# A two-layer encoder on one core: the second sequence's attention norm moved beside the first projection, norms issued in portions, and two pools ordered per layer

## The chip, the cores and the metric

The kernel runs on one core of one Trainium2 chip. Its time is the device time of that core in microseconds, and a version is compared with another by the median of its runs. TensorE is PE in the rows (PEld is its weight load), VectorE is DVE, ScalarE is ACT, GpSimd is POOL, SyncE is SP. A letter q behind an engine's name stands for its queue.

## The reference

Two sequences of 512 tokens, each 1024 wide (`x_prompt` and `x_sample`), go through the same two layers with the same weights; each has a condition vector of its own. In short:

```python
for i in range(2):
    sh1, sc1, g1, sh2, sc2, g2 = adaln(c, mod_w[i], mod_b[i])   # silu(c) @ w + b, six rows
    h = rmsnorm(x, norm1_g[i]) * (1 + sc1) + sh1
    m = retention(h, ...) if i == 0 else attention(h, ...)
    x = x + g1 * m
    h = rmsnorm(x, norm2_g[i]) * (1 + sc2) + sh2
    x = x + g2 * (square(relu(h @ mlp_w1[i])) @ mlp_w2[i])
return rmsnorm(x, final_g)
```

Layer 0's mixer is a retention with 4 heads (keys 256 wide, values 512 wide, with a decay in both directions, a group norm and a gate). Layer 1's is attention with 8 query heads and 2 key/value heads of 128, with a norm and a rotation of queries and keys. The hidden width of the feed-forward part is 4096. All of it is float32.

## The kernel before, in words

Activations lie transposed, as eight tiles of 128 x 512 (features on the partitions, tokens along the free axis). Each float32 operand of a matmul is cut in two: `hi`, its copy in the short format, and `lo`, the rest, so that one product is three matmuls (`mm3`, L221 to L223: hi with hi, hi with lo, lo with hi). `split` (L225) and `load_piece` (L203) make the cuts: ACT copies, DVE subtracts. Weights come in pieces of 128 x 1024 from DRAM on SP's queue into a raw tile and are then cut. One projection of the attention (`Att.proj`) is four pieces, each used in 24 matmuls, into four PSUM banks.

The program is written out in one order by hand, and a scheduler places it on the engines; each engine runs its instructions in the order it got. `issue_after` and `high_priority` bend that order. Generators (`run`, `weave`, `zipped`, `part`) put the parts of one job between the parts of another.

The stages, in order of time:

- **Retention, steps 0 to 7** (L1215 on): head n of sequence s in step 4s + n. Step 3 also makes the norm of sequence 1 (`nm`, 8 modulated tiles, each with a fetch of x on POOL's queue through `xfp`, three tiles), and step 7 the second norm of sequence 0. `nm.a` is the sum of squares, the root and a diagonal; `nm.c` spreads the diagonal with ones (a matmul into a bank); `nm.m` makes the eight modulated tiles. In step 7 they are made by `modulate_keep`, which also writes each to DRAM. Beside all steps the rows of `adaln` are made by dots on DVE (L385), whose weights are fetched on POOL's queue into the pools f2p (8 tiles) and xfp; the two halves of each condition row (`cb`) and the rotation tables also live in f2p. What is left of the dots is done by `flush` at the end of step 7.
- **The wide stage of layer 0** (`wide_stage`, L902): it closes the mixer's pools and opens sf, su, wh (eight cut weight tiles of 2 KB a partition) and sq (three raw tiles of 4 KB), one behind the other in the memory that the mixer's pools and f2p had. With `reuse_waits="tile"` a new tile waits for the old tiles at its place, not for the whole old pool. Its matmuls are those of the feed-forward part, combined over pairs of pieces and the two sequences with seven products in place of eight (`seven`).
- **The attention** (L1299 on): `nm` is the norm of sequence 0, made between the last down projections of layer 0; `p2, p0, p1` are its projections (2 is keys and values, 0 and 1 the queries), `q2, q0, q1` those of sequence 1, and `nm1` the norm of sequence 1. `a0.heads()` and `a1.heads()` run the heads, and `fill` gives each of their steps a piece of other work. Before, `nm1` is made by the filler of `a0.heads()` and q2 and q0 follow in it; q1 stands behind the heads.
- **The wide stage of layer 1**, the last down projections and the final norm.

The banks of PSUM: "a" four, and "m" four outside the attention, where "s" and "t" have two each instead. `mbank()` gives an "m" bank, or an "a" bank where there is no "m". The pool rp holds 48 tiles for cut activations, fp 12 for plain ones.

Of the kernel before, what the change touches and what calls it, by code (L numbers as in the profile page):

```python
# [22 lines left out]
SQ_W = 8  # L23
SQ_RAW = 3
# [6 lines left out]
def kernel(  # L31
# [84 lines left out]
    def bank(t):  # L116
        return ps[t].tile([P, T], F32, tag=t, name="p" + t)

    def mbank():
        return bank("m") if "m" in ps else abank()  # L120

    def ptile():
# [5 lines left out]
    def abank():  # L128
        return psa.tile([P, T], F32, tag="a", name="pa")
# [29 lines left out]
    def bg_until(n):  # L159
        while len(bg) + len(loaded) > n:  # L160
            bg_dot()
            bg_load()
# [9 lines left out]
    def flush():  # L172
        bg_until(0)

    sq = {}
# [72 lines left out]
    def fetch(src, alloc=xtile, eng=nc.gpsimd):  # L248
        t = alloc()
        eng.dma_start(t, src)  # L250
        return t

    class Stats:
# [26 lines left out]
        def spread(self, dg, sb=False):  # L280
            bc = mbank()
            mm(bc, ones, dg, start=True, stop=True)
            if not sb:
                return bc
            bs = ftile()
            act(bs, bc, AF.Copy)
            return bs
# [17 lines left out]
    def stats_of(tiles):  # L305
        st = Stats()
        for x in tiles:
            st.add(x)
        return st
# [69 lines left out]
    modc = {}  # L379
# [520 lines left out]
    wide_pools = ExitStack()  # L900

    def wide_stage(m, st1):  # L902
        mixer.close()
        sq["f"] = wide_pools.enter_context(tc.tile_pool(name="sf", bufs=SQ_F, reuse_waits="tile"))
        sq["s"] = wide_pools.enter_context(tc.tile_pool(name="su", bufs=SQ_SUM, reuse_waits="tile"))
        sq["w"] = wide_pools.enter_context(tc.tile_pool(name="wh", bufs=SQ_W, reuse_waits="tile"))
        sq["p"] = wide_pools.enter_context(tc.tile_pool(name="sq", bufs=SQ_RAW, reuse_waits="tile"))
        nm = Norm(st1, lambda k: m.x[1][k], modc[m.L, 4, 1], modc[m.L, 3, 1], True, keep=hparks[m.L][1])
        m.h[1] = nm.h
        wide = Wide(m, hparks[m.L], hhparks[m.L], lambda i, k: sqtile if i == 6 or (i == 5 and k < 3) else rtile)  # L910
        wide.negate()
        steps = ([("d", 0, i) for i in range(4)] + [("u", 1, f) for f in range(4)]
                 + [("d", 1, i) for i in range(4)])
        load = lambda q: m.w1(0, q[2]) if q[0] == "u" else m.w2(0, q[2])
        hand_over = {0: [nm.a], 1: [nm.c, lambda: nm.m(4)], 2: [nm.m], 3: [lambda: wide.h_fetch(0)],
                     4: [lambda: wide.h_fetch(1)], 5: [lambda: wide.h_forms(0)], 6: [lambda: wide.h_fetch(2)],
                     7: [lambda: wide.h_forms(1)], 8: [lambda: wide.h_fetch(3), lambda: wide.h_forms(2)],
                     9: [lambda: wide.h_forms(3)]}
        w = load(steps[0])
        for n, (kind, s, i) in enumerate(steps):  # L920
            nxt = load(steps[n + 1]) if n + 1 < len(steps) else None
            if kind == "u":
                if i == 0:
                    m.hh[s] = []
                m.up(w, s)
            else:
                m.down(w, i, s, lambda o, s=s: nc.gpsimd.dma_start(park[s][o], m.x[s][o]))
            w = nxt
            for f in hand_over.get(n, ()):
                f()  # L930
        wide_mlp(wide, m)
# [165 lines left out]
    def run(g, n=None):  # L1097
        while n is None or n > 0:
            try:
                next(g)  # L1100
            except StopIteration:
                return
            if n is not None:
                n -= 1
# [19 lines left out]
    r = Ret(0, x0, [])  # L1124
# [28 lines left out]
    for i in range(4):  # L1153
        for t in range(2):
            k = 2 * i + t
# [58 lines left out]
    m = mlps[0]  # L1214
    for step in range(8):  # L1215
        s, n = divmod(step, 4)
        nm = None
        r.scores(n, strip)
        if step == 3:
            with tc.issue_after(first_pool.ins):  # L1220
                s1 = stats_of(fetch(xs[1][k]) for k in range(KD))
            nm = Norm(s1, lambda k: fetch(xs[1][k]),
                      modc[0, 1, 1], modc[0, 0, 1], True)
            r1 = Ret(1, None, nm.h)
        if step == 7:
            nm = Norm(stats_of(fetch(park[0][k]) for k in range(KD)), lambda k: fetch(park[0][k]),
                      modc[0, 4, 0], modc[0, 3, 0], True, keep=hparks[0][0])
            m.h[0] = nm.h
        if step > 0:
            r.v(n)  # L1230
        if nm is not None:
            nm.a()
        r.g(n, [0] if step else [3])
        if nm is not None:
            nm.c()
        r.y(n)
        if nm is not None:
            nm.m()
        if step < 7:
            strip = decay_strip((n + 1) % 4)  # L1240
        if step == 7:
            r.g(n, [1, 2, 3])
        if step < 7:
            nxt = r1 if step == 3 else r
            n1 = (n + 1) % 4
            for t in (ORDER if step else ORDER_FIRST).split():
                i = int(t[1])
                if t[0] == "q":
                    nxt.qk(n1, i)
                elif t[0] == "z":  # L1250
                    r.tz([i])
                else:
                    r.g(n, [i])
            if step == 0:
                flush()
                for ch in (1, 0, 2):
                    mod_chunk(cb, 0, ch, (1,), True)
                for ch in (4, 3, 5):
                    mod_chunk(cb, 0, ch, alt=ch == 5)
                for ch in (1, 0, 2, 3, 4, 5):  # L1260
                    mod_chunk(cb, 1, ch, alt=ch < 5)
            if step < 7:
                pace[0] = PACE[step]
            if step == 2:
                bg_until(80)
            if step == 3:
                bg_until(72)
            if step == 6:
                bg_until(48)
            if step == 3:  # L1270
                r.out(n, lambda o: nc.gpsimd.dma_start(park[0][o], x0[o]))
                r1.x = [fetch(xs[1][k], ptile) for k in range(KD)]
                r = r1
            else:
                r.out(n)
        else:
            m.x[1] = r.x
            m.ups(0, 0, [0])
            r.tz([0, 1])
            m.ups(0, 0, [1])  # L1280
            r.tz([2, 3])
            m.ups(0, 0, [2])
            st1 = Stats()
            r.out(n, lambda o: st1.add(r.x[o]))
            with tc.issue_after(r.last.ins):
                m.x[0] = [fetch(park[0][k], ftile, nc.scalar) for k in range(KD)]
            m.ups(0, 0, [3])
            flush()
    f2_ctx.__exit__(None, None, None)
    wide_stage(m, st1)  # L1290
    st = [Stats(), Stats()]

    def parker(s):
        def after(o):
            st[s].add(m.x[s][o])
            nc.gpsimd.dma_start(park[s][o], m.x[s][o])
        return after

    run(m.downs(7, 0, parker(0)))  # L1299
    nm = Norm(st[0], lambda k: m.x[0][k], modc[1, 1, 0], modc[1, 0, 0], True)  # L1300
    d = m.downs(7, 1, parker(1))
    run(d, 1)
    nm.a()
# [15 lines left out]
    nm1 = Norm(st[1], lambda k: fetch(park[1][k]), modc[1, 1, 1], modc[1, 0, 1], True)  # L1319
    a1 = Att(1, nm1.h, tabs)  # L1320
    p2, p0, p1 = a0.proj(2), a0.proj(0), a0.proj(1)
    q2, q0, q1 = a1.proj(2), a1.proj(0), a1.proj(1)

    def part(g, n):
        for _ in range(n):
            run(g, 1)
            yield

    def zipped(g, h):
        for _ in range(3):  # L1330
            run(h, 1)
            yield
            run(g, 1)
            yield
        run(g)
        run(h, 1)
        yield

    run(p2, 4)
    run(zipped(p2, p0))  # L1340
    run(zipped(p0, p1))

    def fill():
        h1 = nm1.steps(4)
        for i in range(4):
            run(p1, 1)
            run(h1, 1)
            yield
        run(p1)
        run(h1)  # L1350
        yield from part(q2, 4)
        yield from zipped(q2, q0)

    f = fill()
    weave(a0.heads(), f)
    run(f)
    m = mlps[1]
    st = [Stats(), Stats()]
    with tc.issue_after(a0.last.ins):
        run(q0)  # L1360
    o0 = a0.out(park[0], park[2], st[0])
    run(q1, 4)
    run(o0, 1)
    run(q1, 1)
    run(o0, 1)
# [1 line left out]
    nm = Norm(st[0], lambda k: fetch(park[2][k]), modc[1, 4, 0], modc[1, 3, 0], True, keep=hparks[1][0])  # L1367
# [17 lines left out]
    psm_ctx = banks_of(m=4)  # L1385
    psm_ctx.__enter__()
    wide_stage(m, st[1])

    def finish(s, st):
# [7 lines left out]
    st = [Stats(), Stats()]  # L1397
# [161 lines left out]
```

## Time and profile before

| | |
|---|---|
| median of 3 runs | 2591.9 us (2591.0 to 2595.68) |
| the profiled execution | 2592.08 us |
| its span, first to last instruction | 2590.3 us |
| mean granted clock of TensorE | 0.988 |
| PE busy with matmuls | 2505.1 us, 97% |
| DVE, ACT, POOL busy | 77%, 43%, 20% |

A stretch in which PE is busy for less than its length is idle time of PE; a granted clock of 0.50 is the lower of TensorE's two levels (1.2 GHz against 2.4 GHz). Times in rows count from the span's start.

### The profile page before, as it was taken

How to read it: one execution, taken by the hardware profiler on the slowest of the kernel's cores; microseconds unless marked ns; L12 is line 12 of the kernel's file. 1: busy time of each engine (PE TensorE's matmuls, PEld its weight loads, DVE VectorE, ACT ScalarE, POOL GpSimd, SP SyncE). 2: the span in 40 equal slices, each digit the busy share in tenths (PEclk: the TensorE clock that was granted, in tenths of full speed). 3: DMA queues.
4: the chain of work that ended last, by engine and by line, in shares of the span. 5: the costliest groups of instructions: out<-in, count | busy, mean ns of one | idle time of the engine just before them, and what ended most of it. 6: DMA issues, size and time to landing. Idle time of an engine off the chain costs nothing.

```text
span 2590.3 us, 32585 instructions
## 1 busy us (share of the span) xinstructions
PE 2505.1 (97%) x11186; PEld 2048.7 (79%) x11186; DVE 1993.7 (77%) x3800; ACT 1119.1 (43%) x1949; POOL 525.2 (20%) x947
## 2 busy tenths in 40 slices
PE   6999999999999989999999999899999999999998
PEld 4878888778888777888888887688787788888887
DVE  6777687789989778666888876877766767688877
ACT  3333234232333445444533344776754444454423
POOL 2212212231231112221421110000114122142100
PEclk9999999999999999999999999999999999999999
DMA  7544544555556456444754343223347544485423
GB/s 251 191 146 153 169 134 157 192 170 179 161 179 187 152 181 199 163 163 150 246 195 139 124 143 107 66 66 102 92 152 263 165 161 157 153 276 171 143 89 106
DMA packets 133994, 414.00 MB, mean 160 GB/s; under 512 B 21250, under 2 KB 24194, under 8 KB 133828
## 3 DMA queue, kind: packets, MB, share of 16 engines
q0 software_dynamic: 68352, 224.58, 25.8%
q1 hardware_dynamic: 59284, 180.32, 22.3%
q10 hardware_dynamic: 6192, 7.02, 0.8%
q8 instruction: 88, 1.44, 0.2%
q14 instruction: 78, 0.64, 0.1%
HBM read 332.15 MB, written 79.69 MB: 159 GB/s over the span
## 4 chain that ended last, share of the span: by engine, by line
PE 67%; issue 12%; DVE 9%; DMA 6%; POOL 4%; ACT 1%; POOLq 0%; SPq 0%; ACTq 0%; DVEq 0%
PE pm L222 6%; PE pm L223 6%; PE pm L221 6%; PE pa L671 6%; PE pa L669 6%; PE pa L670 6%; PE pa L222 5%; PE pa L223 5%; PE pa L221 5%; PE pm L671 4%; PE pm L670 4%; PE pm L669 4%; DVE junk L385 2%; POOL hhpark L761 1%; DMA f<-in_modw_dram 1%
## 5 line engine op out<-in xcount | busy, mean ns | idle before, releaser
L208 ACT ACTIVATE whi<-raw 128x1024 fp32r<-128x1024 f32 x174 | 183.8, 1058 | 337.5 <-PE pm L222 152.8
L221 PE MATMUL pm<-r,whi 128*128 128x512 f32 x768 | 302.8, 397 | 11.7 <-ACT r L1176 5.8
L222 PE MATMUL pm<-r,whi 128*128 128x512 f32 x768 | 301.0, 392 | 3.4 <-DVE r L316 2.8
L223 PE MATMUL pm<-r,wlo 128*128 128x512 f32 x768 | 300.3, 391 | 0.0
L209 DVE TENSOR_TENSOR wlo<-raw,whi 128x1024 fp32r<-128x1024 f32 x174 | 213.4, 1227 | 100.0 <-ACT whi L208 97.5
L228 ACT ACTIVATE wh<-rawq 128x512 fp32r<-128x512 f32 x228 | 141.9, 629 | 286.1 <-PE pm L670 157.3
L228 ACT ACTIVATE wh<-sum 128x512 fp32r<-128x512 f32 x208 | 129.7, 629 | 279.8 <-PE pa L670 170.8
L669 PE MATMUL pa<-r,wh 128*128 128x512 f32 x624 | 243.0, 389 | 2.5 <-ACT wh L228 2.5
L671 PE MATMUL pa<-r,wh 128*128 128x512 f32 x624 | 243.0, 389 | 2.0 <-DVE wh L229 2.0
L670 PE MATMUL pa<-r,wh 128*128 128x512 f32 x624 | 242.7, 389 | 0.0
L671 PE MATMUL pm<-r,wh 128*128 128x512 f32 x468 | 182.1, 389 | 0.0
L670 PE MATMUL pm<-r,wh 128*128 128x512 f32 x468 | 182.1, 389 | 0.0
L669 PE MATMUL pm<-r,wh 128*128 128x512 f32 x468 | 182.1, 389 | 0.0
L221 PEld LDWEIGHTS pm<-r,whi 128*128 128x128 f32 x768 | 145.7, 190 | 44.4 <-ACT r L1176 6.2
L222 PE MATMUL pa<-wlo,r 128*128 128x512 f32 x440 | 174.9, 397 | 4.7 <-DVE wlo L209 4.7
L221 PE MATMUL pa<-whi,r 128*128 128x512 f32 x440 | 173.3, 396 | 2.8 <-ACT whi L208 1.5
L223 PE MATMUL pa<-whi,r 128*128 128x512 f32 x440 | 174.1, 396 | 0.0
L385 DVE SCALAR_TENSOR_TENSOR junk<-f,f 128x512 bf16<-128x512 f32 x224 | 156.4, 698 | 22.3 <-DMA f<-in_modw_dram 19.3
L222 PEld LDWEIGHTS pm<-r,whi 128*128 128x128 f32 x768 | 145.3, 189 | 35.4 <-DVE r L316 3.7
L229 DVE TENSOR_TENSOR wh<-sum,wh 128x512 fp32r<-128x512 f32 x208 | 141.6, 685 | 39.4 <-ACT wh L228 38.0
L229 DVE TENSOR_TENSOR wh<-rawq,wh 128x512 fp32r<-128x512 f32 x228 | 155.2, 683 | 21.8 <-ACT wh L228 21.5
L223 PEld LDWEIGHTS pm<-r,wlo 128*128 128x128 f32 x768 | 145.0, 189 | 30.4
(277 smaller groups left out, 6008.7 us busy)
## 6 DMA issues: line engine op xcount, KB each, us to landing
rawq<-in_w_dram SPq DMA_DIRECT2D x144, 512.0 KB, 3.9
raw<-in_wri_dram SPq DMA_DIRECT2D x92, 512.0 KB, 3.7
r<-hhpark POOLq DMA_DIRECT2D x142, 256.0 KB, 4.4
f<-in_modw_dram POOLq DMA_DIRECT2D x128, 256.0 KB, 3.5
hhpark<-f POOLq DMA_DIRECT2D x96, 256.0 KB, 2.9
hhpark<-p POOLq DMA_DIRECT2D x88, 256.0 KB, 2.3
xf<-in_modw_dram POOLq DMA_DIRECT2D x80, 256.0 KB, 3.5
raw<-in_wro_dram SPq DMA_DIRECT2D x32, 512.0 KB, 4.0
```

Source lines behind the costliest of these rows:

```text
L208: act(hi, raw, AF.Copy)
L209: ins = tt(lo, raw, hi.bitcast(F32), ALU.subtract)
L221: mm(ps, a[0], b[0], start=first, stop=False)
L222: mm(ps, a[0], b[1], start=False, stop=False)
L223: return mm(ps, a[1], b[0], start=False, stop=last)
L228: split.last = act(hi, src_f32, AF.Copy)
L229: split.dve = tt(lo, src_f32, hi.bitcast(F32), ALU.subtract)
L385: stt(junk, w[hf], 0.5, cb[hf], ALU.mult, ALU.mult, accum_out=a[:, 2 * k + hf:2 * k + hf + 1])
L669: mm(ps, a[0], b[0], start=first and k == 0, stop=False, **more)
L670: mm(ps, a[0], b[1], start=False, stop=False, **more)
L671: mm(ps, a[1], b[0], start=False, stop=k == n - 1, **more)
L761: nc.gpsimd.dma_start(out[i - 1], t)
```

## The change

Five edits.

1. **Pools of the wide stage.** In layer 0 the raw tiles' pool is opened before that of the cut weight tiles; in layer 1 the order stays (cut weight tiles first).
2. **Portions.** In steps 3 and 7 `nm.m` makes three tiles at a time: three after `r.y`, and three more after each of the gates `g1` and `g2` (the last two after the second of them); before, all eight follow `r.y`.
3. **The norm of sequence 0 at the attention's start** makes tiles 2, 4 and 6 with `modulate_pool`: POOL multiplies x with the spread root, ACT makes hi and the full value with scale and bias, DVE subtracts.
4. **`nm1` moves** from the filler of the heads to between the four quarters of p2. Its diagonal and its spread use a "t" bank (`home`).
5. **The heads' filler**: each of the first four steps takes a step of p1's tail and a quarter of q2; then p1's rest, q2's tail zipped with q0, and three quarters of q1. Behind the heads one quarter of q1 is left where four were.

```diff
+    home = []
+
     def mbank():
+        if home:
+            return bank(home[0])
         return bank("m") if "m" in ps else abank()
...
-        sq["w"] = wide_pools.enter_context(tc.tile_pool(name="wh", bufs=SQ_W, reuse_waits="tile"))
-        sq["p"] = wide_pools.enter_context(tc.tile_pool(name="sq", bufs=SQ_RAW, reuse_waits="tile"))
+        for q, bufs in (("w", SQ_W), ("p", SQ_RAW))[::1 if m.L else -1]:
+            sq[q] = wide_pools.enter_context(tc.tile_pool(name="sq" + q, bufs=bufs, reuse_waits="tile"))
...
         r.y(n)
         if nm is not None:
-            nm.m()
+            nm.m(3)
         if step < 7:
             strip = decay_strip((n + 1) % 4)
         if step == 7:
-            r.g(n, [1, 2, 3])
+            for i in (1, 2, 3):
+                r.g(n, [i])
+                nm.m(3)
...
                 else:
                     r.g(n, [i])
+                    if nm is not None:
+                        nm.m(3)
...
-    nm = Norm(st[0], lambda k: m.x[0][k], modc[1, 1, 0], modc[1, 0, 0], True)
+    nm = Norm(st[0], lambda k: m.x[0][k], modc[1, 1, 0], modc[1, 0, 0], True, (2, 4, 6))
...
-    run(p2, 4)
+    run(p2, 1)
+    home.append("t")
+    nm1.a()
+    run(p2, 1)
+    nm1.c()
+    home.clear()
+    nm1.m(4)
+    run(p2, 1)
+    nm1.m()
+    run(p2, 1)
     run(zipped(p2, p0))
     run(zipped(p0, p1))
 
     def fill():
-        h1 = nm1.steps(4)
         for i in range(4):
             run(p1, 1)
-            run(h1, 1)
+            run(q2, 1)
             yield
         run(p1)
-        run(h1)
-        yield from part(q2, 4)
         yield from zipped(q2, q0)
+        yield from part(q1, 3)
...
-    run(q1, 4)
+    run(q1, 1)
     run(o0, 1)
```

## Rows read from the trace of the kernel before

**Rows 1.** The page, part 1: busy us (share of the span) xinstructions.

```profile
PE 2505.1 (97%) x11186; PEld 2048.7 (79%) x11186; DVE 1993.7 (77%) x3800; ACT 1119.1 (43%) x1949; POOL 525.2 (20%) x947
```

**Rows 2.** The waits of PE: us in total, times, longest us.

```profile
PE pm L221 <- ACT wh L228: 6.8, 1, 6.8
...
PE pa L222 <- DVE wlo L209: 4.7, 2, 4.2
```

**Rows 3.** Stretches: length; PE, PEld, DVE, ACT, POOL busy; granted clock; DMA share; GB/s.

```profile
887.30:891.10 3.80, 1.04 (x4) 0.56 (x4) 3.80 (x7) 2.79 (x5) 1.26 (x3) 1.00 0.57 157
891.00:933.00 42.00, 41.97 (x185) 34.65 (x186) 38.20 (x82) 14.90 (x22) 3.23 (x6) 0.96 0.34 105
933.40:940.20 6.80, 0.00 (x0) 0.00 (x0) 0.71 (x2) 1.27 (x3) 0.00 (x0) 0.71 1.00 364
940.20:943.10 2.90, 2.90 (x7) 2.27 (x8) 2.90 (x5) 2.03 (x4) 0.00 (x0) 0.50 0.59 157
1543.50:1562.50 19.00, 13.32 (x55) 10.19 (x54) 18.84 (x30) 11.28 (x17) 3.24 (x6) 0.96 0.30 95
1555.13:1562.00 6.87, 1.19 (x5) 0.68 (x5) 6.87 (x11) 4.89 (x7) 1.08 (x2) 0.92 0.19 48
1562.00:1567.80 5.80, 5.80 (x14) 4.54 (x15) 3.04 (x5) 0.99 (x1) 0.00 (x0) 0.50 0.84 311
1563.00:1633.00 70.00, 68.86 (x305) 56.42 (x304) 39.53 (x85) 30.48 (x81) 0.00 (x0) 0.97 0.38 118
1633.00:1662.00 29.00, 22.40 (x86) 14.62 (x84) 25.13 (x78) 23.84 (x70) 1.08 (x2) 0.82 0.07 18
1639.40:1649.70 10.30, 8.60 (x19) 5.11 (x20) 9.57 (x34) 8.03 (x26) 0.00 (x0) 0.50 0.00 0
1662.00:1760.00 98.00, 97.95 (x488) 79.26 (x489) 73.66 (x178) 74.50 (x176) 3.22 (x6) 1.00 0.20 61
```

**Rows 4.** Timeline of DVE and SP before layer 0's wide stage; last, its raw loads' landing.

```profile
912.54 1.23 DVE L209 TENSOR_TENSOR wlo<-raw,whi 128x1024 fp32r<-128x1024 f32 x1
...
931.88 0.69 DVE L385 SCALAR_TENSOR_TENSOR junk<-f,f 128x512 bf16<-128x512 f32 x1
...
932.61 2.14 SPq L67 DMA_DIRECT2D rawq<-in_w_dram  x3
...
DMA to landing us min/median/max: 3.6/5.5/7.8
```

**Rows 5.** Layer 1's wide start: timeline of SP and DVE, and PE's wait.

```profile
1912.52 1.38 SPq L67 DMA_DIRECT2D rawq<-in_w_dram  x3
...
1956.72 1.28 DVE L229 TENSOR_TENSOR wh<-rawq,wh 128x512 fp32r<-128x512 f32 x2
...
PE pm L223 <- DVE wh L229: 0.8, 1, 0.8
```

**Rows 6.** Groups of PE from 1633 to 1662: busy us, mean ns | idle before, releaser.

```profile
L221 PE MATMUL ps<-r 128*128 128x512 f32 x11 | 6.4, 582 | 3.1 <-ACT p L1045 3.1
```

**Rows 7.** Groups of DVE and ACT from 1543 to 1563, columns as in rows 6.

```profile
L294 DVE SCALAR_TENSOR_TENSOR r<-f,mc,r 128x512 fp32r<-128x512 f32 x8 | 5.9, 740 | 0.0
...
L620 DVE SCALAR_TENSOR_TENSOR p<-pm,mc,p 128x512 f32<-128x512 f32 x5 | 3.7, 741 | 0.0
...
L293 ACT ACTIVATE r<-f,mc 128x512 fp32r<-128x512 f32 x8 | 5.6, 720 | 3.3 <-DVE f L291 3.3
```

**Rows 8.** Lines L1172 and L1178: ns min/median/max, first and last start us.

```profile
L1172 POOL TENSOR_TENSOR rs<-p,f x3: 1256/1263/1279, 36.8 to 39.3; 128x512 f32<-128x512 f32 x3
...
L1178 DVE TENSOR_TENSOR r<-rs,r x7: 682/692/1431, 39.7 to 73.3; 128x512 fp32r<-128x512 f32 x7
```

**Rows 9.** Instructions on tiles f in step 7, 866 to 892; columns as in rows 8.

```profile
L313 DVE SCALAR_TENSOR_TENSOR f<-xf,mc,f x8: 742/750/755, 869.5 to 887.3; 128x512 f32<-128x512 f32 x8
...
L315 ACT ACTIVATE f<-f,mc x8: 707/710/724, 873.8 to 888.7; 128x512 f32<-128x512 f32 x8
...
L316 DVE TENSOR_TENSOR r<-f,r x8: 681/682/693, 875.1 to 890.3; 128x512 fp32r<-128x512 f32 x8
```

## The prediction

> **What bounds the kernel now.** I read the page first: the matmul row of PE is busy for 2505.1 of 2590.3 us [rows 1], so nothing but PE's idle time and its time at the lower clock can be won back. The view of PE's waits then says where that idle time lies: the longest single wait is a matmul of the wide stage waiting 6.8 us for its first weight cut (`wh`, L228), and one of 4.2 us is for a `wlo` (L209) of the first attention projection [rows 2]. The table of stretches prices each place [rows 3]. A stretch's loss is its length less PE's busy time, plus half of the busy time that was run at granted clock 0.50, which is the lower level of 1.2 GHz, since there a matmul takes twice as long.
>
> - Layer 0's wide start, 933.4 to 940.2: PE 0.00 of 6.80 us; then 2.90 us at clock 0.50. Loss 6.8 + 1.45 = 8.2 us.
> - The first attention projection, 1555.13 to 1562.0: PE 1.19 of 6.87 us, then 5.80 us at 0.50. Loss 5.7 + 2.9 = 8.6 us.
> - The first heads of sequence 0, 1633 to 1662: PE 22.40 of 29.00 us, with 8.60 us of it at 0.50 (1639.4 to 1649.7). Loss 6.6 + 4.3 = 10.9 us; right after, 1662 to 1760, PE is full (97.95 of 98.00).
> - The norm of step 7, 887.3 to 891.1: PE 1.04 of 3.80 us, then a mean clock of 0.96 over the next 42 us. Loss 2.8 + 1.7 = 4.5 us.
>
> The change touches all four; other losses stay.
>
> **The wide start: tiles in another order.** Layer 0's raw tiles lie behind sf, su and wh, 30 + 8 + 16 KB into the region that the mixer pools left; that is f2p's memory (xfp 6, wp 32, rawp 8, dp 3.5 KB come before it). f2p holds the condition rows `cb` that every dot of L385 reads. The rows show it: the last dot runs from 931.88 for 0.69 us, to 932.57, and the three raw loads are issued from 932.61 on [rows 4]. So PE pays a whole landing (3.6 to 7.8 us in that stretch). In the new order raw lies at 38 to 50 KB, over rawp, dp and half a KB of one f2p tile; rawp's last reader is the weight cut at 912.54 (1.23 us), so the first two loads can land long before 933. wh moves on to f2p: its first cut waits for the last dot instead, but for nothing behind it. What is late next is one cut, not a load. Layer 1, whose order is not changed, shows that case: its three loads go out at 1912.52, its first `lo` cut is made at 1956.72, and PE waits 0.8 us for it [rows 5]. I take that 0.8 us: 6.8 - 0.8 = 6.0 us, and the 1.45 us of the clock: **-7.4 us**. Bounds: 8.2 (nothing left) and 0 (the cut and a late load meet as before).
>
> **The heads: sequence 1's projections as filler.** Before, the filler of heads 0 to 2 is p1's tail and the norm of sequence 1, and neither has large matmuls; PE therefore waits for the softmax chain (`ps` waits 3.1 us for the exponentials of L1045) [rows 6]. After, a quarter of q2, 24 matmuls, stands in each of the first four filler steps. From 891 to 933 185 matmuls take 41.97 us [rows 3], 0.227 us each, so q2 is 4 x 5.4 = 22 us of work that waits for nothing in the heads, against a hole of 6.6 us. From 1662 on the same heads run with projections beside them and PE idles 0.05 us in 98. What remains is the start: q2 needs the banks that p1's four copies free. I leave 1.5 us for that: 6.6 + 4.3 - 1.5 = **-9.4 us**. q1's three quarters, now in a0's heads, replace q2's at the tail; PE's work is only moved. Bounds: 10.9, and 0 if the heads' own chain is the limit (DVE is busy 25.13 and ACT 23.84 of 29 us there).
>
> **The norm of sequence 1, moved beside p2.** Eight modulations, two DVE instructions each of 0.74 us (L291 like L294) [rows 7], are 11.8 us, on ACT eight of 0.72 us. The root and the diagonal are a dozen instructions on four columns and one full one, which I put at 2 us. From 1563 to 1633 DVE is busy 39.53 of 70.00 us [rows 3], so 53.4 after: it fits. It issues no new DMA: the five fetches of `xf` that remain behind three made early move up in POOL's queue, in a stretch where POOL runs nothing (0.00 us). But DVE runs in order, and a modulation that waits for its fetch holds the weight cuts behind it. In step 7 eight modulations with fetches, from the first L313 at 869.5 to the last L316 at 890.3, spread over 21.5 us [rows 9]; at 8 x (0.75 + 0.68) = 11.4 us of DVE work, some 10 us of that was waiting and other work. Bounds 0 and +10; the cuts stand up to four weight buffers of 5.4 us ahead, so I take **+1 us**. The bank: with `home` the diagonal and spread use "t", which nothing else uses before k's transposes; 0.
>
> **POOL in three modulations.** k = 2, 4, 6 give up 2 x 0.74 us of DVE for one subtraction of 0.68 us [rows 7, 9]: 3 x 0.80 = 2.4 us less, in a stretch where DVE is busy 18.84 of 19.00 us and its backlog is what the 5.7 us gap waits for. In exchange POOL multiplies, 1.26 us each, and ACT does three more of 0.71 us [rows 8, 9] (it has 7.7 us free in those 19). The rows have a price for DVE as well: beside the one like multiplication a subtraction took 1.43 us instead of 0.69 [rows 8]. Three times 0.74 us is 2.2 us back, so I take **0** for the sum, between -3.9 (2.4 us and half of the 2.9 us of clock) and +1.4 (three whole multiplications, 3.8 us, on DVE's path).
>
> The Trainium skill (SBUF — State Buffer, "Who interferes with whom") says that a VectorE instruction with two SBUF inputs and a GpSimd instruction that reads SBUF exclude each other for a whole instruction. The 1.43 us row agrees, and so taken without exception the rule would make this edit +1.4 us and the whole 2577.7.
>
> **Norms in portions.** In step 3 PE has no wait that a portion would end: 0. In step 7 up to 4.5 us could come back, but the gate evacuations now go ahead of the last modulations on DVE (three of 0.68 us, so up to 2 us later), and whatever PE wins there meets the dots: DVE is busy 38.20 of 42 us from 891 to 933, and the first wide cut cannot be made before the last dot. I take 0; bounds -4.5 and +2.
>
> **Sum.** The profiled execution took 2592.08 us (span 2590.3 and 1.8 around it; the median of the three runs is 0.2 us less). 2592.1 - 7.4 - 9.4 + 1.0 = 2576.3, so **2576 us**.
>
> **The rivals.**
> 1. *The edits at p2 and step 7 pay too* (2569). POOL's products fall beside DVE instructions that read PSUM (L620, five of 0.74 us in those 19), 3.9 us less, and step 7 gives back some 3 of its 4.5 us. For it: ACT and POOL have room. Against it: the 1.43 us row and the dots. Chance 0.2.
> 2. *The heads are bound by their own chain* (2586). DVE and ACT at 87% and 82% from 1633 to 1662: q2's matmuls fill PE, but the heads end no earlier and PE starves at their tail. Against it: from 1662 to 1760 they are busy only 75% and 76% with PE full. 2576 + 9.4. Chance 0.14.
> 3. *The wide start only trades waits* (2584): the third raw tile touches a `cb` tile, loads are issued in order, the cut is made late. 2576 + 7.4; against it stands layer 1. Chance 0.1.
> 4. *Slower* (2600): in-order DVE. If each late modulation holds p2's and p0's cuts, the whole norm, about 21.5 us as spread in step 7 and 2 us of chain, comes onto PE's path: 2576 + 24. It decides when more than 21 us reach PE, that is, when the four buffers of cuts (22 us) give no cover at all. Chance 0.05.
> 5. *POOL excludes DVE throughout* (2578), as above. Chance 0.08, and inside the forecast's range.
>
> **How the numbers follow.** The forecast itself, 2576 with 2571 to 2581 around it, gets 0.43. From 2565 to 2586 all cases but half of the second, the fourth and the best end of the first are held, about 8 in 10. A measurement of this kernel tells 0.2%, 5.2 us, from no change. Below 2586.7: the forecast, rivals 1, 3, 5 and most of 2, so 0.87 faster; 0.09 the same; 0.04 slower.
>
> **What would show it.** Right: in the wide start of layer 0 the raw loads go out before 920 and PE's gap is under 1.5 us at full clock; from 1633 to 1662 PE is busy over 27 us, with `pa` matmuls of q2 between the heads; the first `wlo` of p2 still comes 3 to 6 us late. Wrong: raw loads that still start with the last dot; `xf` fetches named in DVE's waits between 1563 and 1633 with PE idle there; PE idle at the end of a0's heads or at the start of a1's, where q1's 16 us no longer stand.

## The result, and the profile after

The changed kernel takes 2568.2 us at the median (four runs, 2566.7 to 2568.8) where the kernel before took 2591.5 in the same measurement: a ratio of 0.9912 (95% interval 0.9900 to 0.9924), 23.3 us less. Measured once more with the experiments it took 2571.0 us (six runs, 2564.6 to 2576.8), a ratio of 0.9924 (0.9907 to 0.9940). The forecast was 2576, with 2565 to 2586 around it.

The page, part 1, of the changed kernel:

```profile
span 2566.6 us, 32586 instructions
...
PE 2499.5 (97%) x11186; PEld 2047.6 (80%) x11186; DVE 1997.1 (78%) x3797; ACT 1122.4 (44%) x1952; POOL 530.3 (21%) x950
```

PE has as many matmuls as in [rows 1]; 5.6 us less busy time at the same count goes with less time at the lower clock (mean granted clock 0.991, before 0.988); another 18 us are idle time that is gone. The waits of PE, as in [rows 2]:

```profile
PE pt L274 <- DVE f L268: 2.8, 1, 2.8
PE pa L673 <- ACT wh L232: 2.7, 3, 1.2
PE pm L225 <- ACT wh L232: 2.4, 1, 2.4
...
PE pa L225 <- ACT f L983: 2.3, 1, 2.3
```

The 6.8 us at the wide start have become 2.4 (`pm`, L225, on `wh`), and no `wlo` is left among the long waits. Two new ones stand in the first projection: the matmul of `nm1`'s sum (`pt`, L274) waits for the last square, and p0's first matmul for a bank that ACT copies out (L983). The table of stretches, columns as in [rows 3]; the first answers to 933.4 to 940.2, the last to 1633 to 1662, the others lie in the first projection:

```profile
930.68:933.03 2.35, 0.00 (x1) 0.00 (x1) 0.54 (x1) 1.17 (x3) 0.00 (x0) 1.00 1.04 403
...
1554.08:1556.92 2.84, 0.00 (x0) 0.03 (x1) 2.84 (x6) 2.84 (x5) 0.58 (x1) 0.89 0.71 183
1556.92:1566.73 9.81, 9.81 (x34) 8.19 (x35) 7.18 (x17) 1.19 (x2) 0.00 (x0) 0.69 0.53 163
...
1577.52:1579.81 2.29, 0.00 (x0) 0.00 (x1) 2.06 (x4) 2.15 (x3) 0.54 (x1) 1.00 0.60 174
1579.81:1590.32 10.51, 10.51 (x39) 8.54 (x40) 7.96 (x22) 6.79 (x25) 0.54 (x1) 0.84 0.51 151
...
1629.74:1658.74 29.00, 29.00 (x142) 23.19 (x141) 25.87 (x70) 23.76 (x68) 0.00 (x0) 1.00 0.16 43
```

The first heads are full: 29.00 of 29.00 us at clock 1.00, with 142 matmuls where 86 ran in [rows 3]. In the first projection PE still idles 2.8 and 2.3 us, each followed by a stretch with half clock in it.

One profile is not enough to price the edits: stretches that hold the same instructions differ between executions. So the kernels below are compared by stretches between two of PE's matmuls, counted from its first: A, matmuls 600 to 2400 (in the kernel before from 171 to 587 us, with step 3's norm); B, 3400 to 3730 (step 7's norm); C, 3730 to 4130 (the last output of the retention and the wide start); D, from 6530 to the first score matmul of sequence 0 (the last down projections, p2, p0, p1); E, from there to the first score matmul of sequence 1, which is matmul 7608 in every kernel (the heads of sequence 0); F, from there to the last matmul. Each number is the difference of two start times in that kernel's trace, in us. Where `nm1` stands beside p2, D holds ten matmuls more and E ten fewer, those of `nm1`'s sum and spread; where PE does not wait, they take 1.3 us together. The ratios are to the kernel before as run beside each (medians 2590.3 to 2591.5).

| kernel | median us | ratio to before (95%) | A | B | C | D | E | F |
|---|---|---|---|---|---|---|---|---|
| before | 2591.5 | | 416.3 | 82.6 | 99.6 | 92.6 | 155.8 | 793.5 |
| changed | 2568.2 | 0.9912 (0.9900 to 0.9924) | 414.7 | 79.8 | 96.3 | 94.9 | 140.9 | 790.0 |
| changed, again | 2571.0 | 0.9924 (0.9907 to 0.9940) | 410.7 | 83.8 | 94.1 | 93.4 | 140.8 | 789.9 |
| old filler | 2571.8 | 0.9930 (0.9918 to 0.9942) | 417.7 | 82.8 | 95.1 | 94.7 | 141.0 | 789.6 |
| old pool order | 2579.2 | 0.9957 (0.9943 to 0.9971) | 415.7 | 84.2 | 100.5 | 94.3 | 140.9 | 793.2 |
| no portions | 2571.9 | 0.9927 (0.9914 to 0.9940) | 416.7 | 83.8 | 93.5 | 93.6 | 140.8 | 792.5 |
| no POOL products | 2577.0 | 0.9943 (0.9930 to 0.9956) | 412.9 | 84.6 | 97.8 | 96.9 | 140.9 | 793.5 |
| before + `nm1` moved | 2579.2 | 0.9956 (0.9944 to 0.9969) | 416.2 | 81.9 | 100.2 | 96.9 | 141.1 | 790.2 |
| before + pool order | 2586.0 | 0.9979 (0.9970 to 0.9987) | 415.2 | 83.3 | 97.8 | 92.4 | 155.8 | 791.8 |
| before + POOL products | 2590.3 | 0.9994 (0.9982 to 1.0006) | 415.9 | 83.2 | 100.8 | 91.6 | 155.8 | 793.5 |
| q2 held back | 2591.1 | 0.9998 (0.9989 to 1.0007) | 416.4 | 82.0 | 94.5 | 94.9 | 160.1 | 793.0 |
| `nm1` later | 2568.1 | 0.9912 (0.9898 to 0.9926) | 414.5 | 84.5 | 95.1 | 89.8 | 141.4 | 796.3 |
| `nm1` later still, a fetch moved | 2565.0 | 0.9892 (0.9876 to 0.9909) | 415.3 | 85.3 | 93.7 | 85.3 | 141.5 | 793.7 |
| the same, a diagonal later | 2561.5 | 0.9884 (0.9868 to 0.9901) | 413.5 | 84.0 | 95.2 | 85.7 | 141.4 | 790.2 |

The reader should see first how much a stretch moves where nothing in it was changed: among the nine kernels with portions A lies between 410.7 and 417.7, B between 79.8 and 85.3, and F differs by 6.4 us between the changed kernel run again and the one with `nm1` later. F has one wait of 2.1 us, for the sum that the diagonal of sequence 0's second norm needs, in all profiles but the last. In four of these thirteen no stretch at the lower clock follows it, and F is 789.6 to 790.2; in the nine others one does, and F is 791.8 to 796.3. Without the wait F is 790.2. Around the wait PE ran like this in the changed kernel, and with POOL's products taken out:

```profile
1830.00:1855.00 25.00, 22.75 (x114) 16.89 (x113) 21.75 (x55) 20.35 (x40) 4.04 (x8) 1.00 0.28 85
```

```profile
1838.00:1863.00 25.00, 22.75 (x99) 17.10 (x99) 19.04 (x49) 17.45 (x35) 2.70 (x5) 0.86 0.19 59
```

The same wait, once with no half clock behind it and once with clock 0.86 and 15 matmuls fewer in the 25 us. So 3.5 of the 23.7 us between the spans of the two first profiles (F), and B's 2.8, can be put down to no edit.

### The profile page after: what moved, and what is told of

Read it like the earlier page. It is cut to its first block, busy times and chain, and to the rows that moved or that the text cites. A ratio compares the mean times of both kernels' runs of the same rounds, so it can differ in the third digit from the quotient of the medians.

```text
span 2566.6 us, 32586 instructions
## 1 busy us (share of the span) xinstructions
PE 2499.5 (97%) x11186; PEld 2047.6 (80%) x11186; DVE 1997.1 (78%) x3797; ACT 1122.4 (44%) x1952; POOL 530.3 (21%) x950
## 4 chain that ended last, share of the span: by engine, by line
PE 74%; issue 8%; DVE 7%; DMA 5%; POOL 3%; ACT 2%; ACTq 0%; SPq 0%; POOLq 0%; DVEq 0%
PE pm L226 7%; PE pm L227 6%; PE pm L225 6%; PE pa L675 6%; PE pa L673 6%; PE pa L674 6%; PE pa L225 5%; PE pa L226 5%; PE pa L227 5%; PE pm L675 5%; PE pm L674 5%; PE pm L673 5%; DVE junk L389 1%; DVE wlo L213 1%; PE pt L1066 1%
## 5 line engine op out<-in xcount | busy, mean ns | idle before, releaser
L225 PE MATMUL pm<-r,whi 128*128 128x512 f32 x768 | 304.5, 399 | 12.0 <-ACT r L1180 5.2
L225 PEld LDWEIGHTS pm<-r,whi 128*128 128x128 f32 x768 | 146.6, 191 | 45.5 <-ACT r L1180 5.6
L225 PE MATMUL pa<-whi,r 128*128 128x512 f32 x440 | 176.9, 403 | 2.3 <-ACT f L983 2.3
```

The source lines that it names most:

```text
L225: mm(ps, a[0], b[0], start=first, stop=False)
```

## Experiments

**Each edit undone in the changed kernel.** The old filler, with `nm1` still beside p2:

```diff
         for i in range(4):
             run(p1, 1)
-            run(q2, 1)
             yield
         run(p1)
+        yield from part(q2, 4)
         yield from zipped(q2, q0)
-        yield from part(q1, 3)
...
-    run(q1, 1)
+    run(q1, 4)
```

> The changed kernel (2568.2 us) with the old filler: nm1 stays beside p2, but q2 comes after p1's tail and q1 stands wholly behind the heads. Theory (q2's matmuls fill the hole of the first heads): PE idles again in the first heads, 6.6 us and a half-clock stretch worth 4.3, so 2579 us, and PE shows gaps of 1 us and more in the first 30 us of the heads. Rival (the heads gained because nm1's work left DVE and ACT, not because q2 came): 2568 to 2570 us, PE full in the heads as in the changed kernel.

Measured 2571.8, against 2571.0 for the changed kernel. The theory, which was the prediction's, falls: PE is full in the first heads with the old filler too. Its stretch, 29 us from the first scores on:

```profile
1632.40:1661.40 29.00, 29.00 (x142) 23.16 (x142) 25.77 (x70) 23.61 (x67) 0.00 (x0) 1.00 0.15 42
```

The same 142 matmuls. Of them 67 write `pa` banks. The matmuls of p2, p0 and p1 all stand ahead of the first scores, so these are projections of sequence 1, between the heads although the filler names them later. The heads are issued under `high_priority`, and the scheduler sets whatever is ready behind them into PE's order. The order in which the filler lists the work did not decide here.

The pool order, undone (`(("w", SQ_W), ("p", SQ_RAW))` for both layers):

> The changed kernel with the raw tiles behind the cut tiles in both layers. Theory: the raw loads again wait for the last dot, which now ends some 3 us earlier because of the portions, and PE's gap at the wide start of layer 0 grows from 2.4 to 6 or 7 us with a half-clock stretch behind it: 2572.5 us (the 4.4 us that the stage gained). Rival 1 (the whole 7.4 us of the prediction belongs to the pools and something else took 3 back): 2575.5 us. Rival 2 (the order only trades waits): 2568 to 2569 us.

2579.2, above all three; stretch C is 100.5 us, 5.2 more than the mean of the ten kernels with the new order (95.3), and F is 3.2 over the changed kernel's, in code that the edit doesn't touch. Of the place itself, the gap and what followed:

```profile
932.88:939.62 6.74, 0.01 (x2) 0.01 (x1) 0.72 (x2) 1.28 (x3) 0.00 (x0) 0.77 0.99 364
939.62:942.60 2.98, 2.98 (x7) 2.36 (x8) 2.98 (x5) 2.03 (x4) 0.00 (x0) 0.50 0.54 151
```

That is [rows 3] again, within 0.1 us, with every other edit in place.

The old order shows in p2 as well, which the forecast did not have. ACT's first two weight cuts there (`whi`) stand ahead of the modulations in all ten kernels with the new order, and behind most of them in the four with the old one; no run shows why. Here with the old order, then in the changed kernel:

```profile
1558.12 1.04 ACT L212 ACTIVATE whi<-raw 128x1024 fp32r<-128x1024 f32 x1
```

```profile
1538.25 2.00 ACT L212 ACTIVATE whi<-raw 128x1024 fp32r<-128x1024 f32 x2
```

PE's waits for the first cuts follow both this order and POOL's products: old order without the products, 1.5 us for a `whi` and 4.2 or 4.1 for a `wlo` (two kernels); old with them, 4.8 for a `whi` (two); new without them, 5.9 for a `wlo` (two); new with them, none of 1 us or more (eight). The length of D does not follow the pool order: 94.3 us here, and 94.3 in the mean of the five kernels with the new order, POOL's products and the same place of `nm1`.

The portions, undone (`nm.m()` behind `r.y`, none behind the gates):

> The changed kernel with all eight tiles of the norms in steps 3 and 7 behind r.y again. Theory (the portions take 1.7 us of PE's wait out of step 3 and 2.8 us out of step 7): 2572.7 us, with PE's gaps near 489 and 887 as long as before. Rival (what the portions win in step 7 meets the dots, and step 3's difference is only where the lower clock fell): 2568 to 2570 us, with the wide start's gap longer by what step 7's is shorter.

2571.9: no difference, the rival. Over all kernels, B is 83.4 us with portions (mean of nine) and 82.9 without (five), A 414.6 and 416.1, where the nine spread over 7 us.

POOL's products, undone (the tuple `(2, 4, 6)` left out):

> The changed kernel with the eight modulations ahead of p2 all on DVE. Theory (POOL takes 2.4 us off DVE's backlog and gives about 2.2 back, since one DVE sum took 2.47 us and one weight cut 1.65 us beside POOL's products in the changed kernel): 2567 to 2570 us, no difference that can be told. Rival 1 (the edit pays): 2570.5 to 2572 us, the first matmul of nm1's sum in p2 later by 2 us. Rival 2 (POOL's products cost more than they take off): 2565 to 2567 us.

2577.0, above every range: D is 96.9, 2.6 over those five kernels (94.3); the rest of the 6 us lies where this edit has no instruction (C, F, and 2 us between C and D). PE's waits in p2 without them, where the changed kernel has none for a `wlo`:

```profile
PE pa L226 <- DVE wlo L213: 5.9, 1, 5.9
PE pa L225 <- ACT f L983: 2.1, 1, 2.1
```

And DVE's order, first without the products, then in the changed kernel (start, us):

```profile
1544.12 2.74 DVE L295 SCALAR_TENSOR_TENSOR f<-f,mc 128x512 f32<-128x512 f32 x4
...
1559.16 1.22 DVE L213 TENSOR_TENSOR wlo<-raw,whi 128x1024 fp32r<-128x1024 f32 x1
1560.29 0.69 DVE L268 TENSOR_TENSOR f<-f 128x512 f32<-128x512 f32 x1
1560.89 1.22 DVE L213 TENSOR_TENSOR wlo<-raw,whi 128x1024 fp32r<-128x1024 f32 x1
```

```profile
1540.51 1.65 DVE L213 TENSOR_TENSOR wlo<-raw,whi 128x1024 fp32r<-128x1024 f32 x1
...
1548.12 2.47 DVE L268 TENSOR_TENSOR f<-f 128x512 f32<-128x512 f32 x1 [0.78 <-ACT f L267]
1550.51 1.21 DVE L213 TENSOR_TENSOR wlo<-raw,whi 128x1024 fp32r<-128x1024 f32 x1
```

Without POOL the first cut comes behind all the modulations, at 1559; with it two cuts stand among them, at 1540.5 and 1550.5. DVE did not get 2.4 us back: a sum took 2.47 us (0.68 elsewhere) and a cut 1.65 (1.21) while POOL multiplied, 2.2 us in all. What it got is another order. That the order is what pays is not shown: with the old pool order, where the first `wlo` comes at 1560.0 behind most modulations, POOL's products shorten D by the same 2.6 us (96.9 with `nm1` moved alone, 94.3 in the changed kernel with the old order).

**Yardstick.** The changed kernel with no edit:

> The changed kernel once more, unedited, as the yardstick for the others. Theory (its stretches ahead of step 7 move by some 2 us from one execution to the next, since the waits in steps 3 and 7 end with transfers of the background dots, whatever PE gained before them): a median between 2567 and 2571 us, with PE's wait ahead of the diagonal of step 7 anywhere from 1.8 to 4 us. Rival (the first four executions are exact, and each kernel's waits are its own): 2568 us within 1, the waits of steps 3 and 7 as in its first profile.

2571.0, the upper end of the theory's range; the wait ahead of step 7's diagonal was 2.7 us, 1.8 in the first profile.

**One edit alone, in the kernel before.** First `nm1` (edit 4, with `home`), without q2 in the first filler steps:

```diff
-    run(p2, 4)
+    run(p2, 1)
+    home.append("t")
+    nm1.a()
...
+    nm1.m()
+    run(p2, 1)
...
-        h1 = nm1.steps(4)
         for i in range(4):
             run(p1, 1)
-            run(h1, 1)
             yield
         run(p1)
-        run(h1)
```

> The kernel before (2590 to 2592 us) with nm1 alone moved beside p2; filler otherwise as before, no q2 in the first four steps. Theory (formed after the run with the old filler, which kept PE full in the first heads: what counts is that nm1's tiles are there before the heads, so that q2's matmuls are ready and the scheduler places them in the holes): the 10.9 us of the first heads go, and some 2 us come on in p2, so 2579 to 2582 us. Rival (the prediction's: the filler has to hold q2): the hole of the first heads stays, 2590 to 2593 us.

2579.2, the theory. E falls from 155.8 to 141.1 us, as far as with all five edits; D rises from 92.6 to 96.9. Together they are 10.5 us shorter. From the start of the heads:

```profile
1641.00:1670.00 29.00, 29.00 (x143) 23.19 (x141) 25.78 (x70) 23.61 (x67) 0.00 (x0) 1.00 0.15 43
```

The pool order alone:

> The kernel before with the new order of the two pools in layer 0 alone. Theory (the order alone ends the late loads, what was left of the wait in the changed kernel, 2.4 us, is ACT's evacuation ahead of the first cut): 2585.5 to 2587 us, PE's gap at the wide start 1.3 to 2.5 us. Rival (the prediction's term): 2584 us, gap under 1 us. Second rival (without the portions the dots end later, and the first cut waits for them): 2588 to 2590 us, gap over 4 us.

2586.0, 5.4 us of 2591.5 by the ratio, as the first theory had it; the gap is 2.1 us, at full clock (start 932.79), so neither rival.

POOL's products alone:

> The kernel before with POOL in three of the modulations ahead of p2, alone. Theory (what the stretch of p2 lost with POOL taken out of the changed kernel, about 2.5 us, and a shorter half-clock stretch behind it): 2586 to 2589 us, the wait for the first wlo under 3 us where it was 4.2. Rival (the prediction's sum: DVE gets back what POOL takes off): 2590 to 2592 us, the wait as long as before.

2590.3: no difference that can be told, the prediction's sum. D is 1.0 us less: in p2 PE waits 4.8 us once, for a cut of ACT's, where it was 5.7 us in two waits (1.5 and 4.2). The second row is DVE's sum beside POOL:

```profile
PE pa L221 <- ACT whi L208: 4.8, 1, 4.8
```

```profile
1553.36 3.25 DVE L264 TENSOR_TENSOR f<-f 128x512 f32<-128x512 f32 x1
```

**Is it q2's matmuls, or `nm1`'s work leaving DVE and ACT?** The old filler, and q2's matmuls alone held back:

```diff
                 w = piece(wai[c, i])
+                with tc.issue_after(self.hold.ins) if c == 2 and self.s else nullcontext():
...
         run(p1)
+        a1.hold = a0.last
         yield from part(q2, 4)
```

> The changed kernel with the old filler (2571.8 us), and q2's matmuls, not its loads and cuts, held back until the second head's last matmul; nm1 stays beside p2. Theory (the norm's early place pays because it gives the scheduler ready matmuls for the first heads): PE idles there again, and the stretch from the first scores on is longer by 8 to 11 us, 2580 to 2583 us. Rival (it pays because nm1's work on DVE and ACT has left the heads): PE's idle time there stays under 2 us, 2570 to 2574 us.

2591.1: as slow as the kernel before, although `nm1` stands beside p2 as in the changed kernel. The rival falls; the theory's size was too small, E is 160.1 us, 19 more than with q2 free. PE's stretch, and what its score matmuls waited for:

```profile
1629.48:1658.48 29.00, 20.58 (x63) 13.54 (x63) 21.48 (x65) 19.57 (x60) 0.00 (x0) 0.71 0.05 19
```

```profile
PE ps L225 <- ACT p L1050: 7.2, 8, 1.4
```

This is the hole of [rows 3, 6], deeper: 63 matmuls, clock 0.71, the same wait for the exponentials. In the kernel before 86 matmuls ran in the same length: ten of `nm1`, three of q2 at the very end, and ten more of the heads' own.

**Better places.** `nm1`'s sum one quarter of p2 later, its modulations behind p2's matmuls and in p0:

```diff
-    run(p2, 1)
+    run(p2, 2)
     home.append("t")
     nm1.a()
     run(p2, 1)
     nm1.c()
     home.clear()
-    nm1.m(4)
-    run(p2, 1)
-    nm1.m()
     run(p2, 1)
+    nm1.m(4)
     run(zipped(p2, p0))
+    nm1.m()
```

> The changed kernel with nm1's sum and diagonal one quarter of p2 later, and its modulations behind p2's last matmuls and in p0. Theory (PE waits 2.84 us for nm1's last square and 2.29 us for a bank whose copy ACT makes late behind nm1's modulations, and each wait is followed by a stretch at half clock): both waits go, up to 5.1 us and 4.7 of the clock, 2560 to 2563 us. Rival (the wait is DVE's backlog from the last down projection, and the next weight cut is late in place of the square): 2566 to 2569 us, with a wait for a wlo cut near 1560.

2568.1, between the two, and not told apart from the changed kernel by the medians. D says more: 89.8 us, 4.5 less than the mean of 94.3. The two waits were gone, but a new one of 3.1 us stood before `nm1`'s spread (L286), not before a cut; F was 6.4 us longer than the yardstick's, in code that the edit leaves alone. So the spread went behind all four quarters as well (`run(p2, 2)`, `nm1.a()`, `run(p2, 2)`, `nm1.c()`), and at the wide start the last of the eight fetches went to POOL's queue:

```diff
-[fetch(park[0][k], ftile, nc.scalar) for k in range(KD)]
+[fetch(park[0][k], ftile, nc.scalar if k < 7 else nc.gpsimd) for k in range(KD)]
```

> The changed kernel (2571.0 us in the same job as the run with nm1 later) with nm1's sum behind two quarters of p2, its spread behind all four, its first modulations there and the rest in p0; and the last of the eight fetches on ACT's queue at the wide start moved to POOL's. Theory (each of PE's waits in p2 is nm1's place in PE's order and nothing else; the wide start waits for ACT, which waits with that fetch): no wait over 1 us in p2, under 1.2 us at the wide start, 2563 to 2566 us. Rival (DVE's backlog: a wlo cut is late instead): 2568 to 2571 us, a wait of 2 us or more in p2.

2565.0, in the theory's range. D is 85.3 us, and the first projection has no gap (stretch of 44 us):

```profile
1546.00:1590.00 44.00, 44.00 (x197) 36.14 (x196) 38.19 (x80) 23.99 (x48) 6.38 (x9) 1.00 0.48 149
```

At the wide start the wait is 1.3 us, where the theory had under 1.2; it is 1.4 in the changed kernel's second profile, and 1.3 in three kernels with the fetch where it was, so moving it is worth nothing that can be told. Last, one more `yield` in the filler of the second sequence's heads, between `o0` and `nm.steps(4)`:

> The same, with the diagonal of the second norm of sequence 0 one step of the filler later in the second sequence's heads, where PE waits 2.14 us for the last square in every profile so far, with 0 to 3.2 us of half clock behind it. Theory: that wait goes, 2559 to 2564 us. Rival (PE then waits at the next place for the same sum): the time of the run without this step.

2561.5: that wait is 0.6 us instead of 2.1. The ratio of this version, 0.9884 (0.9868 to 0.9901), lies below the interval of the changed kernel measured with the experiments; it is the fastest of all here, by the median 9.5 us under the changed kernel run again and 29.4 under the kernel before as run beside it. Its last step touches none of the five edits, and is not told apart from the run without it (2565.0) by the ratios.

## Why the prediction was right, and where it was not

The range held the time, and "faster" was right. The likeliest value was 5 to 8 us too high, and one of its two large terms stood on the wrong edit.

- **The heads (-9.4).** Right in place: the hole that was read from [rows 3] is full, its 6.6 us of idle time and 4.3 us of lower clock are gone. The step that failed is "the heads: sequence 1's projections as filler", the reason given. With the old filler the gain is the same; with `nm1` moved alone it is there; with q2 held back it is gone. What was missing before was not a place in the list, but q2's input: as long as `nm1` is made in the heads, no q2 matmul is ready there. The 1.5 us kept back for the start of q2 were not needed. All of E lost 14.9 us, 4.0 beyond the bound of 10.9: some 1.8 of these are `nm1`'s ten matmuls, which left with it (2.65 us there, part of it at the lower clock and counted above), and the rest is not broken down.
- **`nm1` beside p2 (+1.0).** Within its bounds, and too low: done alone it made D 4.3 us longer. Of these 1.3 us are its ten matmuls, which the sum had nowhere; PE's idle time in D went from 6.8 to 8.2 us; and a second stretch of 3.4 us at the lower clock cost 1.7. The mechanism was another, too: the forecast looked at DVE and the fetches of `xf`; what the changed kernel's trace shows is PE itself, in order, at `nm1`'s sum (2.8 us) and ACT, in order, with the bank's copy behind `nm1`'s modulations (2.3). The runs with `nm1` later took 4.5 and then 9.0 us out of D, so the place, not the amount of work, held them.
- **The wide start (-7.4).** The mechanism was right: the first raw load goes out at 905.6 (932.61 in [rows 4]) and the gap has full clock; the second goes out only at 927.2, where the forecast had the raw loads out before 920. The size was off: -5.0 by C (means of all kernels with either order), -5.4 alone. The wait left was set at 0.8 us by layer 1's start [rows 5]; it measured 1.3 to 2.4. In seven of the ten kernels with the new order PE also waits 1.0 to 2.2 us some 45 us later, for a `lo` cut of `wh`; with the old order that is so in one of four. Here the first cut stands in ACT's order behind other work, eight fetches that ACT issues, the last of them late, and the copy of a retention bank; the last dot had ended at 929.86. Where the copy starts as soon as its matmul has ended, with that fetch moved away or not, the wait is still 1.3 us, so the copy and the cut behind it are what is left; a run with the cut first was not made. ACT's timeline there, in the changed kernel:

```profile
926.62 5.14 ACTq L254 DMA_DIRECT2D f<-park  x8
931.86 0.60 ACT L613 ACTIVATE f<-pm 128x512 f32<-128x512 f32 x1 [4.62 <-DMA f<-park]
932.36 1.14 ACT L232 ACTIVATE wh<-rawq 128x512 fp32r<-128x512 f32 x2
```

- **POOL (0, between -3.9 and +1.4).** Right alone, within what can be told; and the 2.2 us back on DVE that it summed from [rows 8] are what the changed kernel's trace shows. The Trainium skill (SBUF — State Buffer, "Who interferes with whom") says that such a sum and such a product shut each other out; the sums of 2.47 and 3.25 us agree. Beside `nm1` in p2 the edit took 2.6 us out of D, a term set at zero, with either pool order. DVE's order of cuts and modulations differs between the two pool orders and the gain does not, so the cause of these 2.6 us stays open. The sign that the first `wlo` of p2 "still comes 3 to 6 us late" did not come: with the new pool order and POOL's products no cut is waited for there.
- **Portions (0).** Right within what can be told: B is no shorter with them, A 1.5 us shorter in the mean with a spread of 7.
- **The sum.** C -5.0, E -15.0, D +1.5 make -18.5, near the 20.1 us of the second measurement; the forecast had -15.8. What the first measurement had beyond that lies in B and F, where the clock and the transfers differ from execution to execution.

Of the rivals, the first came nearest in its number (2569), but in part by luck: POOL's products gave 2.6 of its 3.9 us, step 7 gave nothing that can be told, and the heads gave more than its sum had. The fourth, held cuts, did not come; the heads' own chain was no limit with PE at 29.00 of 29.00 us.

## What to carry to other kernels

Where a scheduler fills an engine's holes with whatever is ready, ask which input makes the work ready, and move that; the order of the filler may be worth nothing. A small reduction moved beside a large product costs by the places of its few instructions in the in-order queues, so put its matmul where its operand is surely done, and its evacuations behind the ones that free a bank. And price edits by stretches between the same two instructions in several executions, with a look at what work stands between them in each kernel: here stretches with the same code moved by 5 to 7 us, more than three of the five edits were worth.

## What was not expected of the hardware

A DVE sum of two SBUF tiles (0.68 us) that started at 1548.12, when POOL's first product was ending, took 2.47 us and ended 0.56 us after POOL's second product, which began later than the sum did:

```profile
1546.87 1.30 POOL L303 TENSOR_TENSOR f<-f 128x512 f32<-128x512 f32 x1
1548.12 0.58 POOL L1304 DMA_DIRECT2D park<-p  x1
1548.72 1.31 POOL L303 TENSOR_TENSOR f<-f 128x512 f32<-128x512 f32 x1
```

By these start times the instruction that came first was the one that was held. In the changed kernel's second profile the sum started after the first product had begun and took 3.1 us, again to 0.56 us after the end of the second. The profile's spans on POOL are rough, and no run tested this alone. And the same wait of 2.1 us was followed by no half clock in the changed kernel and by 6.9 us at clock 0.51 in the version with `nm1` later still (below, right behind the wait), where half of that time is lost: the wait cost 2.1 us or 5.5, and no run shows what decides.

```profile
1830.42:1837.30 6.88, 6.88 (x21) 5.77 (x22) 4.16 (x16) 2.24 (x6) 0.54 (x1) 0.51 0.37 114
```
